# Making the low halves of every expert's weights on VectorE instead of sharing them with GpSimd

## The chip, the cores and the metric

The kernel runs on one core of a Trainium2 chip. The metric is the device time of one execution in microseconds (us). The core's engines run side by side and each works through its own instructions in order: TensorE (PE, with its weight loads shown as PEld), VectorE (DVE), ScalarE (ACT), GpSimd (POOL) and SyncE (SP), which issues most of the DMA transfers. GpSimd also issues the indirect transfers, that is the gathers and the scatter-additions by a list of rows.

## The reference, cut to what matters

The reference is one layer: two token mixers, then a mixture of experts, then a final norm. Only the experts bear on the change. 1024 tokens each go to 2 of 32 experts, and every expert is a SwiGLU of width 512 on rows of 1024:

```python
def expert_block(args):
    xb, e = args
    return (jax.nn.silu(xb @ w_gate[e]) * (xb @ w_up[e])) @ w_down[e]

y_buf = lax.map(expert_block, (x_buf, blk_e)).reshape(n_slots, d)
out = jax.ops.segment_sum(y_buf.astype(f32) * w_buf[:, None], tok_buf, num_segments=n_tok + 1)
```

All of it is in float32. Every expert's weights are read once, 6 MB each.

## The kernel before, in words

Up to about 690 us of the profile the kernel does the mixers, the output projection and the routing. What follows is the expert stage, and it ends at about 1330 us; the final norm comes last.

The stage walks 32 places, one expert each. Fifteen of them are **half experts**: they are given to experts that have at most 64 rows here, and their matmuls take the float32 weights as they came from memory (`half_gu` at L1263, `half_down` at L1287). One more half block rides along with place 13. The other seventeen places are **full experts** of 128 rows. From place 3 on, half and full ones mostly take turns. A full expert's product is made of three products of reduced-precision halves: a weight tile `wf` is split into a high part `wh` (ACT copies it, L181) and a low part `wl` (the source less the high part, L182), and PE multiplies high by high, high by low and low by high (`gu` at L1322, `down` at L1348). The rows `xT` and the hidden `hT` are split in the same way (L1312, L1341).

A full expert's weights come in twelve parts of 128 x 1024: parts 0 to 7 are gate and up, 8 to 11 are down. `chunk` (L1406 and on) hands one part out and has it split; `w_split` and `split` do it. In the kernel before, the low parts of 8 and 10 are made on POOL and all the others on DVE; `ON_POOL = (8, 10)` sets that, and the last place is left out of it. That is two instructions at each of 16 full experts, 32 in all. The tiles `wh` and `wl` have four buffers each, so a new part waits until PE has read the one four parts back.

Rows come in by a gather: POOL issues an indirect DMA that fills `xe` (L1239 for a full expert, L1234 for a half one), PE transposes it (`pxe`, L1309 and L1252) and ACT copies it out. `xe` has two buffers. The result `ye` or `yeh` (DVE, L1354 and L1292) is added into memory by another indirect DMA of POOL (L1358 and L1296). So POOL's queue in this stage holds, in an order that a scheduler fixes when the program is built: gathers, additions and the 32 low parts, and each waits for all before it. The order of `schedule` sets which step of which expert comes next; the scheduler then interleaves the engines' instructions by what it expects to be ready. DVE's queue holds the low parts, the products `hg` and `hgh` of the SwiGLU (L1330, L1270), the low halves of rows and hidden, a small helper for half experts' row numbers (`hrow`, L1202), and the results. SP loads the weights ahead into thirteen buffers of 1 MB, each as soon as one is free (L1218), and the row lists `lst` (L1200).

Of the kernel before, what the change touches and what calls it, by code (L numbers as in the profile page):

```python
# [25 lines left out]
NE = 32  # L26
# [34 lines left out]
H = 64  # L61

TS = NT + P

ON_POOL = (8, 10)


def ranks():
# [58 lines left out]
class Kern:  # L127
# [1282 lines left out]
    def chunk(self, p, part):  # L1410

        self.prefetch(len(self.order))
        c, h = self.part_of(part)
        f, s = self.F[p, c]
        if h:
            del self.F[p, c]
            self.live[s] -= 1
        f = f[:, h * D:(h + 1) * D]
        return f, None if self.half(p) else self.w_split(f, self.nc.gpsimd if part in ON_POOL and p < NE - 1 else None)

    def moe(self):
        blocks = list(range(MID + 1)) + [NE] + list(range(MID + 1, NE))
# [72 lines left out]
    def moe_rest(self):  # L1495
# [24 lines left out]
        with self.tc.For_i(0, n) as i:  # L1520
            ev, rv = self.ovf_regs(i)
            nc.sync.dma_start(out=lst, in_=self.tab[bass.ds(rv, P), :])
            self.gather(0, lst)
            x = self.x_t(0, (xh, xl), pt)
            for j in range(8):
                w = chunk(ev, j)
                self.gu(j // 2, x, w, w, pg, (j % 2,))
            h = self.act(pg, sg, hg)
            self.h_t(h, hT, pt)
            for f in range(4):  # L1530
                self.down(hT, chunk(ev, 8 + f), py, f)
            self.y_add(self.y_out(py, lst, y), lst)
# [193 lines left out]
```

## Time and profile before

| | |
|---|---|
| median of 3 runs | 1360.84 us (1359.11 to 1360.85) |
| the profiled execution | 1360.35 us |
| its span, first to last instruction | 1358.3 us |
| TensorE clock granted, mean | 0.94 |
| PE busy over the span | 1180.0 us (87%) |
| DVE busy | 842.5 us (62%) |
| ACT busy | 598.7 us (44%) |
| POOL busy | 430.7 us (32%) |

The profiled execution's own time is 2.05 us over its span; that is what lies before the first and behind the last instruction. It is 0.49 us below the median of the runs. Times in the views are us from the span's start. A row of a timeline gives the start, the length, the engine, the line, the operation and its tiles, and, in square brackets, how long the engine sat idle before it and what released it. Rows that follow each other with equal operations are merged (x2, x3). A row of the stretches gives each engine's busy time with its count of instructions, the granted TensorE clock as a share of full speed, the share of time the DMA engines were busy, and the rate of all transfers.

### The profile page before, as it was taken

What the parts mean: (1) busy time and instruction counts of PE and PEld (TensorE: products, weight loads), DVE (VectorE), ACT (ScalarE), POOL (GpSimd) and SP (SyncE); (2) the same over time, 40 slices, a digit from 0 to 9 for tenths busy, and PEclk for the clock granted to TensorE, in tenths of its full rate; (3) what the DMA queues carried; (4) which work ended last, traced back from release to release, by engine and by line L of the source; (5) the groups of instructions that cost most, each with busy time, mean ns of one, the idle gap of its engine ahead of it and who ended that gap; (6) DMA issues with size and microseconds to landing.
All of it is one profiled execution on the core that took longest, in us unless ns stands there. A gap on an engine that the chain in (4) does not pass through costs nothing. (4 is left out here: it accounts for less than half of the span.)

```text
span 1358.3 us, 18814 instructions
## 1 busy us (share of the span) xinstructions
PE 1180.0 (87%) x6628; PEld 859.1 (63%) x6628; DVE 842.5 (62%) x1364; ACT 598.7 (44%) x1064; POOL 430.7 (32%) x322
## 2 busy tenths in 40 slices
PE   5899999888888999899838999887999988898882
PEld 2678778788886666688726656454556655555552
DVE  1688884778858877556577754454555545454455
ACT  5633322455367766433425543332344333334344
POOL 0340001476523444013333431333332333332230
PEclk9699999979898999999968999899999989998996
DMA  9765645766223300873466999998689999988955
GB/s 333 252 207 167 209 136 160 248 195 213 93 79 121 109 9 16 298 260 130 167 224 228 347 387 406 367 347 323 240 328 402 398 357 327 376 339 319 342 176 231
DMA packets 104480, 335.02 MB, mean 247 GB/s; under 512 B 19532, under 2 KB 37964, under 8 KB 79808
## 3 DMA queue, kind: packets, MB, share of 16 engines
q1 hardware_dynamic: 94672, 314.78, 62.8%
q0 software_dynamic: 9136, 17.36, 5.2%
q10 hardware_dynamic: 576, 1.66, 0.3%
q8 instruction: 53, 0.87, 0.2%
q14 instruction: 43, 0.35, 0.1%
HBM read 299.74 MB, written 43.43 MB: 253 GB/s over the span
## 5 line engine op out<-in xcount | busy, mean ns | idle before, releaser
L182 DVE TENSOR_TENSOR wl<-wf,wh 128x1024 fp32r<-128x1024 f32 x172 | 255.8, 1518 | 121.4 <-ACT wh L181 121.2
L181 ACT CAST wh<-wf 128x1024 fp32r<-128x1024 f32 x204 | 204.7, 1050 | 146.5 <-PE pgu L1322 96.5
L1263 PE MATMUL pgu<-wf,xT 128*64 128x256 f32 x1024 | 136.0, 391 | 0.4 <-DVE yeh L1292 0.4
L182 POOL TENSOR_TENSOR wl<-wf,wh 128x1024 fp32r<-128x1024 f32 x32 | 87.3, 2738 | 84.7 <-ACT wh L181 74.1
L1322 PE MATMUL pgu<-wl,xh 128*128 128x512 f32 x272 | 98.1, 425 | 16.5 <-DVE wl L182 16.3
L1322 PE MATMUL pgu<-wh,xh 128*128 128x512 f32 x272 | 97.9, 434 | 9.9 <-ACT wh L181 9.8
L1263 PEld LDWEIGHTS pgu<-wf,xT 128*64 128x64 f32 x1024 | 72.0, 138 | 50.8 <-issue 16.4
L468 PE MATMUL pzq<-xw,hxh 128*128 128x256 f32 x512 | 100.1, 295 | 0.0
L770 POOL TENSOR_SCALAR p<-p,sst 128x640 f32<-128x640 f32 (+1 forms) x32 | 66.1, 2065 | 101.4 <-DVE sst L767 53.7
L1322 PE MATMUL pgu<-wh,xl 128*128 128x512 f32 x272 | 89.5, 410 | 0.0
L1348 PE MATMUL py<-wh,hT 128*128 128x512 f32 x272 | 83.5, 414 | 4.9 <-ACT hT L1340 3.1
L468 PEld LDWEIGHTS pzq<-xw,hxh 128*128 128x128 f32 x512 | 83.1, 196 | 1.0 <-issue 0.2
L1322 PEld LDWEIGHTS pgu<-wl,xh 128*128 128x128 f32 x272 | 54.1, 199 | 39.9 <-DVE wl L182 26.8
L1322 PEld LDWEIGHTS pgu<-wh,xh 128*128 128x128 f32 x272 | 51.2, 198 | 40.7 <-ACT wh L181 26.1
L349 PE MATMUL pxb<-hxh,xw 128*128 128x512 f32 x256 | 76.4, 397 | 0.0
L468 PE MATMUL pzq<-xw,hxl 128*128 128x256 f32 x256 | 74.2, 290 | 0.0
L1296 POOL DMA_INDIRECT acc<-yeh,hrow x16 | 34.6, 2160 | 121.2 <-DVE yeh L1292 102.8
L753 DVE TENSOR_REDUCE sst<-psc 128x1 f32<-128x640 f32 (+1 forms) x64 | 50.4, 789 | 27.7 <-PE psc L752 22.8
L1348 PEld LDWEIGHTS py<-wh,hT 128*128 128x128 f32 x272 | 49.7, 193 | 26.1 <-issue 6.7
L1287 PE MATMUL py<-wf,hTh 128*64 128x512 f32 x256 | 63.3, 614 | 0.9 <-ACT hTh L1280 0.9
L1322 PEld LDWEIGHTS pgu<-wh,xl 128*128 128x128 f32 x272 | 54.4, 200 | 13.4 <-issue 2.4
L1358 POOL DMA_INDIRECT acc<-ye,lst x16 | 35.0, 2185 | 87.5 <-DVE ye L1354 77.2
(348 smaller groups left out, 2559.1 us busy)
## 6 DMA issues: line engine op xcount, KB each, us to landing
wf<-in_w_gate SPq DMA_DIRECT2D x64, 1024.0 KB
wf<-in_w_up SPq DMA_DIRECT2D x64, 1024.0 KB
wf<-in_w_down SPq DMA_DIRECT2D x64, 1024.0 KB
wa<-in_w_ada SPq DMA_DIRECT2D x48, 512.0 KB
R<-csd SPq DMA_DIRECT2D x16, 512.0 KB
xl<-xd SPq DMA_DIRECT2D x17, 256.0 KB
xt<-in_x SPq DMA_DIRECT2D x8, 512.0 KB
xf<-in_w_xbc SPq DMA_DIRECT2D x8, 512.0 KB
```

Source lines behind the costliest of these rows:

```text
L181: self.nc.scalar.copy(hi, src)
L182: (eng or self.nc.vector).tensor_tensor(lo, src, hi.bitcast(F32), OP.subtract)
L349: nc.tensor.matmul(px[s], w(wp, kc), self.hx(hp, kc, s, 512), start=st, stop=sp)
L468: nc.tensor.matmul(ps, self.hx(hp, kc, b // 4, P, (b % 4) * P), w(wp, kc), start=kc == 0 and hp + wp == 0, stop=kc == KC - 1 and hp == 1)
L753: v.tensor_reduce(mx, ps[:, o:512 + nl], AX.X, OP.max)
L770: (v if j % 2 else nc.gpsimd).tensor_scalar(p_, p_, den[:, j - i:j - i + 1], None, op0=OP.mult)
L1263: self.nc.tensor.matmul(pg[n * H:n * H + H, o:o + 256], xT[:, i0 + kk, a * H:a * H + H], w[:, kk * 512 + n * 256:kk * 512 + n * 256 + 256] ...
L1287: self.nc.tensor.matmul(py[n * H:n * H + H, 0:512], hT[:, i, a * H:a * H + H], w[:, n * 512:n * 512 + 512], start=f == 0, stop=f == 3)
L1296: self.nc.gpsimd.indirect_dma_start(out=self.acc.rearrange("t (a c) -> (t a) c", a=2), out_offset=bass.IndirectOffsetOnAxis(ap=self.hrow[: ...
L1322: nc.tensor.matmul(pg[:, n * 512:(n + 1) * 512], x[xp][:, k, :], w[wp][:, kk * 512:(kk + 1) * 512], start=k == 0 and xp + wp == 0, stop=k ...
L1348: nc.tensor.matmul(py[:, n * 512:(n + 1) * 512], hT[:, hp, f, :], wd[wp][:, n * 512:(n + 1) * 512], start=f == 0 and hp + wp == 0, stop=f ...
L1358: self.nc.gpsimd.indirect_dma_start(out=self.acc[:, :], out_offset=bass.IndirectOffsetOnAxis(ap=lst[:, 0:1], axis=0), in_=y, in_offset=Non ...
```

## The change

`ON_POOL` goes, and every full expert's low parts are made on DVE:

```diff
-
-ON_POOL = (8, 10)
...
-        return f, None if self.half(p) else self.w_split(f, self.nc.gpsimd if part in ON_POOL and p < NE - 1 else None)
+        return f, None if self.half(p) else self.w_split(f)
```

`w_split` hands its `eng` on to `split`, which uses `self.nc.vector` when it is None. Two lines go at the top, so every line number of the changed kernel is lower by two. ACT's instructions keep their order, SP's differ by the place of one register load, and on PE a few of the rows' transposes move ahead by some matmuls. On POOL 32 instructions go; on DVE 32 come, and the scheduler places the others around them anew.

The first place is POOL, at one full expert between two half experts in the second half of the stage. Before, the queue holds a half expert's gather (`hrow`) and addition (`yeh`), the two low parts, the next full expert's gather (`lst`) and this one's addition (`ye`):

```order
L1234 DMA xe_6890<-h2d,hrow 128x512
L1296 DMA acc<-yeh,hrow 2304x512
L182 TENSOR_TENSOR wl<-wf,wh 128x1024 x2
L1239 DMA xe_6889<-h2d,lst 128x1024
L1358 DMA acc<-ye,lst 1152x1024
L1234 DMA xe_6890<-h2d,hrow 128x512
```

In the changed program the same place reads:

```order
L1232 DMA xe_6890<-h2d,hrow 128x512
L1294 DMA acc<-yeh,hrow 2304x512
L1237 DMA xe_6889<-h2d,lst 128x1024
L1356 DMA acc<-ye,lst 1152x1024
L1232 DMA xe_6890<-h2d,hrow 128x512
```

The full expert's gather has moved up: it now stands right behind the half expert's addition, with nothing between.

The second place is DVE, at the first full expert of the stage's second half, from a half expert's result (`yeh`) to the full expert's down parts. Before:

```order
L1292 SCALAR_TENSOR_TENSOR yeh<-py,lst,g2h 128x512
L182 TENSOR_TENSOR wl<-wf,wh 128x1024 x2
L1330 TENSOR_TENSOR hg<-sg,pgu 128x512
L182 TENSOR_TENSOR wl<-wf,wh 128x1024
L1341 TENSOR_TENSOR hT<-phT,hT 128x512
L182 TENSOR_TENSOR wl<-wf,wh 128x1024 x3
```

And in the changed program:

```order
L1290 SCALAR_TENSOR_TENSOR yeh<-py,lst,g2h 128x512
L180 TENSOR_TENSOR wl<-wf,wh 128x1024 x4
L1328 TENSOR_TENSOR hg<-sg,pgu 128x512
L180 TENSOR_TENSOR wl<-wf,wh 128x1024
L1339 TENSOR_TENSOR hT<-phT,hT 128x512
L180 TENSOR_TENSOR wl<-wf,wh 128x1024 x3
```

Parts 8 and 10 have come in ahead of `hg`, which now waits for four low parts where it waited for two.

## The prediction

> **What bounds the kernel now.** I read the page first, then the waits of PE in the expert stage, then the timelines of POOL, DVE and PE around the longest of them.
>
> ```profile
> PE 1180.0 (87%) x6628; PEld 859.1 (63%) x6628; DVE 842.5 (62%) x1364; ACT 598.7 (44%) x1064; POOL 430.7 (32%) x322
> ```
>
> PE is busiest by far, so a wait counts if PE sits in it. These are PE's own in the expert stage, 720 to 1350 us (total, times, longest):
>
> ```profile
> PE pxe L1309 <- DMA xe<-h2d,lst: 19.8, 8, 3.8
> PE pgu L1322 <- DVE wl L182: 13.1, 15, 1.3
> PE pgu L1322 <- ACT wh L181: 9.8, 7, 1.4
> PE phT L1338 <- DVE hg L1330: 6.7, 4, 2.9
> PE pxe L1252 <- DMA xe<-h2d,hrow: 4.4, 1, 4.4
> PE py L1348 <- POOL wl L182: 4.1, 7, 1.2
> ...
> PE py L1348 <- DVE hT L1341: 1.6, 4, 0.5
> ```
>
> The largest is not a weight part at all: eight times PE stands before a full expert's rows, which a gather of POOL brings. The next fences show why it is late, in the cycle from 1115 to 1160 us: POOL, then SP's load of the gather's row list, then the transposes on PE that read the rows.
>
> ```profile
> 1123.86 2.32 POOL L1296 DMA_INDIRECT acc<-yeh,hrow  x1 [7.76 <-DVE yeh L1292]
> 1132.05 5.76 POOL L182 TENSOR_TENSOR wl<-wf,wh 128x1024 fp32r<-128x1024 f32 x2 [5.87 <-ACT wh L181]
> 1137.95 1.86 POOL L1239 DMA_INDIRECT xe<-h2d,lst  x1
> ```
>
> ```profile
> 1097.72 0.33 SPq L1200 DMA_DIRECT2D lst<-tab  x1
> ...
> 1106.50 1.10 PE L1309 MATMUL pxe<-C,xe 128*128 128x128 f32 x4 [3.79 <-DMA xe<-h2d,lst]
> ...
> 1122.83 0.75 DVE L1292 SCALAR_TENSOR_TENSOR yeh<-py,lst,g2h 128x512 f32<-128x512 f32 x1 [4.74 <-PE py L1287]
> ...
> 1123.50 3.49 DVE L182 TENSOR_TENSOR wl<-wf,wh 128x1024 fp32r<-128x1024 f32 x3
> ```
>
> ```profile
> 1147.47 0.75 PE L1309 MATMUL pxe<-C,xe 128*128 128x128 f32 x4 [2.25 <-DMA xe<-h2d,lst]
> ```
>
> ```profile
> 1160.93 0.75 DVE L1292 SCALAR_TENSOR_TENSOR yeh<-py,lst,g2h 128x512 f32<-128x512 f32 x1 [4.65 <-PE py L1287]
> ```
>
> The gather is issued at 1137.95, the moment the two low parts are done; POOL had been idle for 5.87 us ahead of them, waiting for ACT's high parts. It takes 9.52 us until PE is released (1147.47 - 1137.95). Its buffer was read out by the transposes that start at 1106.50, and its list was asked for at 1097.72.
>
> **The change part by part.** *The gathers.* With the low parts gone, the gather stands right behind the addition, which ends at 1123.86 + 2.32 = 1126.18. Nothing else that it needs is later: the transposes that free the buffer begin 20 us before, and the list was asked for 28 us before. Landing 9.52 us on, it is there at 1135.70, and PE wants it at 1147.47 - 2.25 = 1145.22. The spare is 9.52 us, more than twice the longest wait of 3.8. Behind the gather in POOL's queue stand the addition and the next half expert's gather; each comes sooner, not later. I take all 19.8 us off; next late there is the high part from ACT, which PE waits for already (9.8 in all) and which stays.
>
> *The clock.* The granted clock falls after these waits. The stretches begin where PE resumes after a gather, except the second, which follows the wait for `hg`:
>
> ```profile
> core 0: us, PE busy (x) PEld busy (x) DVE busy (x) ACT busy (x) POOL busy (x), PEclk, DMA share, GB/s
> 865.00:877.00 12.00, 10.31 (x36) 6.50 (x37) 4.84 (x5) 5.20 (x6) 1.05 (x1) 0.72 0.91 331
> ...
> 1018.00:1025.00 7.00, 4.56 (x18) 2.87 (x19) 4.21 (x4) 0.59 (x1) 0.70 (x1) 0.76 1.02 418
> 1106.00:1118.00 12.00, 10.06 (x31) 6.16 (x31) 4.75 (x5) 5.20 (x6) 1.04 (x1) 0.59 0.78 297
> 1147.00:1159.00 12.00, 9.60 (x44) 6.11 (x44) 4.85 (x5) 5.37 (x7) 1.04 (x1) 1.00 0.98 345
> 1185.00:1197.00 12.00, 9.50 (x36) 5.77 (x37) 4.85 (x5) 5.20 (x6) 0.96 (x1) 0.86 0.91 325
> 1226.00:1238.00 12.00, 10.15 (x32) 6.40 (x33) 4.79 (x5) 5.20 (x6) 0.00 (x0) 0.61 0.93 335
> 1267.00:1279.00 12.00, 9.61 (x36) 5.84 (x37) 4.72 (x4) 5.20 (x6) 0.00 (x0) 0.86 1.02 377
> ```
>
> Clock lost behind gathers is 12 us times one less the clock: 3.4 + 4.9 + 1.7 + 4.7 + 1.7 = 16.4 us. Not all of it is time, since PE also waits there for parts. The same work, from the transposes to `yeh`, took 1122.83 - 1106.50 = 16.33 us at a clock of 0.59 and 1160.93 - 1147.47 = 13.46 at 1.00: 2.87 us for 4.9 us of lost clock, a ratio of 0.59. So 16.4 x 0.59 = 9.6 us. The bounds are nothing (the halving comes back behind other waits) and 16.4.
>
> The Trainium skill (TensorE: Matmul & The Clock Gate, Part 1: The HAM clock gate) says the clock halves after an idle window of about 3.4 us. By that only the waits of 3.79 and the one at 1226 would cost clock, and this term would be (4.9 + 4.7) x 0.59 = 5.6 us, the sum 4 us less; the row at 1185 speaks against it, for the clock fell there too.
>
> *The low parts.* On DVE a low part costs 1.22 us where POOL is quiet, and beside POOL it stands still:
>
> ```profile
> 1009.89 1.22 DVE L182 TENSOR_TENSOR wl<-wf,wh 128x1024 fp32r<-128x1024 f32 x1
> 1014.38 5.40 DVE L182 TENSOR_TENSOR wl<-wf,wh 128x1024 fp32r<-128x1024 f32 x1 [3.27 <-ACT wh L181]
> 1019.71 0.68 DVE L1330 TENSOR_TENSOR hg<-sg,pgu 128x512 f32<-128x512 f32 x1
> ```
>
> ```profile
> 1013.97 4.73 POOL L182 TENSOR_TENSOR wl<-wf,wh 128x1024 fp32r<-128x1024 f32 x2
> ```
>
> ```profile
> 1015.10 1.05 ACT L181 CAST wh<-wf 128x1024 fp32r<-128x1024 f32 x1 [0.74 <-PE pgu L1322]
> ```
>
> ```profile
> L182 DVE TENSOR_TENSOR wl<-wf,wh 128x1024 fp32r<-128x1024 f32 x164 | 246.1, 1532 | 121.4 <-ACT wh L181 121.2
> ...
> L182 POOL TENSOR_TENSOR wl<-wf,wh 128x1024 fp32r<-128x1024 f32 x32 | 87.3, 2738 | 84.7 <-ACT wh L181 74.1 <-issue 10.5
> ```
>
> One DVE part took 5.40 us while POOL made two in 4.73. Over the stage DVE's mean is 1532 ns, 0.31 us over 1.22, so 164 x 0.31 = 51 us of DVE time is standing beside POOL. The change adds 32 x 1.22 = 39 us to DVE and takes up to 51 off. For PE what counts is when the down parts are ready: POOL's pair takes 5.76 us, all four on DVE 4 x 1.22 = 4.88. So the 4.1 us that PE waits for POOL's parts goes, and what would be late next, the hidden's low half (1.6), is no later; I count its gain as nothing, 1.6 at most.
>
> *`hg`.* It now stands behind four low parts at two full experts. At the first of these, the last of the four needs ACT's part, done at 1015.10 + 1.05 = 1016.15; then 1.22 and 0.68 give 1018.05, against 1019.71 + 0.68 = 1020.39 before. That is 2.3 us of the 2.9 us wait, and the 7 us stretch behind it lost 1.7 us of clock, x 0.59 = 1.0. Nothing to 6.7 bounds it with its like.
>
> *The rest.* The half expert's gather (4.4) waits for `hrow` on DVE; I leave it, with 0 to 4.4 as bounds. The three full experts in a row at the start are where DVE is fullest:
>
> ```profile
> 720.00:770.00 50.00, 46.45 (x207) 34.63 (x205) 38.05 (x31) 31.89 (x37) 21.98 (x11) 0.97 0.82 299
> ...
> 838.00:960.00 122.00, 103.59 (x522) 64.73 (x523) 58.53 (x53) 44.16 (x58) 41.13 (x20) 0.96 0.94 352
> ```
>
> ```profile
> 1014.00:1090.00 76.00, 72.16 (x387) 46.48 (x386) 43.66 (x40) 32.25 (x43) 24.31 (x12) 0.98 1.02 398
> 1100.00:1262.00 162.00, 139.17 (x682) 88.23 (x680) 78.70 (x73) 59.74 (x76) 53.12 (x24) 0.93 0.91 340
> ```
>
> In 720 to 770 DVE would go from 38.05 to at most 38.05 + 6 x 1.22 = 45.4, just under PE's 46.45: nothing, 7.3 us of loss at worst. From 1100 on DVE has 83 of 162 us free.
>
> Sum: 19.8 + 9.6 + 4.1 + 2.3 + 1.0 = 36.8 us off the profiled execution's 1360.35 us, which is 0.5 below the median: 1323.5, said as 1323.
>
> **The rivals.** *The gather stays late* (0.12). DVE now runs low parts closer together while POOL prepares its transfers, or the gather meets the addition's own transfer ahead of it. Beside DVE's three parts the addition at 1123.86 took 2.32 us. The delay decides only beyond the 9.52 us of spare, and the run of DVE parts that could hold it is four, 4.88 us. If it does, 19.8 + 9.6 are lost: 1360.35 - 7.4 = 1353.
>
> *The weight stream becomes the bound* (0.10). From 1100 to 1262 transfers move 340 GB/s x 162 us = 55.1 MB. My terms there, the waits before 1106.50, 1147.47 and two more of that size, some 12 us, and 11.3 x 0.59 = 6.7 of clock, leave 143 us, so 385 GB/s are wanted. The row from 1014 to 1090 held 398 at a share of 1.02, for 76 us. If only the midpoint of 340 and 398 is kept, 369, the stretch takes 149, 6 us more; 838 to 960, with 352 already, loses about as much: 1323.5 + 12 = 1335, up to 1340. The Trainium skill (SBUF — State Buffer, A bandwidth-pool intuition that's wrong (but worth ruling out)) gives about 358 GB/s from memory to a core; by it the stretch would take 154 us and the sum come to some 1340. The measured 398 decides against it.
>
> *DVE sets the pace* (0.04), the slower side. If two more low parts per full expert make the down parts late, each costs 1.22 on PE's path: 32 x 1.22 = 39 us and, with the gather gain failing, 1399. It decides where four DVE parts take longer than POOL's pair, that is above 5.76 / 4 = 1.44 us each. Rows without POOL show 1.22, and DVE's 83 free us speak against it.
>
> *Nothing comes of it* (0.04). The low parts are gone from POOL, so the change does what it says; but the gained time could be given back at the next wait for high parts: 1360.
>
> **How the numbers follow.** The forecast has 0.70. Its own range, with the clock term from 0 to 16.4, the other waits' bounds and a small part of the 7.3, is 1311 to 1333. The stream rival carries the upper end to 1340; outside are the late gather, DVE's pace and nothing, together 0.20. A measurement of this kernel can tell about 0.2%, 2.7 us, from no change. Faster: 0.70 + 0.12 + 0.10 = 0.92; same 0.04; slower 0.04.
>
> **What would show it.** In the changed profile: DVE's low parts x196 in the stage at a mean near 1.22 us, none on POOL; the wait of the transposes for the gathered rows near zero; the clock at 1.00 behind them; the second half of the stage at a DMA share near 1.0. Wrong would be a wait for rows that stays, a new wait of PE for low parts above 13.1 us, or high parts waiting for weights.

## The result, and the profile after

The changed kernel takes 1315.54 us in the median of 4 runs (1313.18 to 1322.09). The kernel before, run beside it, takes 1359.97 us (1352.35 to 1360.85). The ratio is 0.9694, with a 95% interval of 0.9655 to 0.9734. The profiled execution takes 1317.32 us at a span of 1315.2 us, against 1360.35 and 1358.3: 43.0 us less, where the prediction's sum said 36.8. In the changed file the lines behind the removed two are two lower: the low part is L180, the high part L179, the gather of a full expert L1237, its transposes L1307.

The page of the changed kernel, busy times:

```profile
PE 1164.3 (89%) x6628; PEld 853.0 (65%) x6628; DVE 828.8 (63%) x1396; ACT 598.2 (45%) x1064; POOL 341.2 (26%) x290
```

DVE has 32 instructions more and is busy 13.7 us less (842.5 before). How, the groups of instructions show; DVE's low parts from 720 to 1310 us of the changed kernel (count, busy, mean in ns):

```profile
L180 DVE TENSOR_TENSOR wl<-wf,wh 128x1024 fp32r<-128x1024 f32 x195 | 230.8, 1220 | 85.6 <-ACT wh L179 82.3 <-DMA wf<-in_w_down 2.4
```

195 low parts at a mean of 1220 ns; before, 164 took 1532 ns each. Now PE's waits in the same stretch (total, times, longest):

```profile
PE pgu L1320 <- DVE wl L180: 13.7, 17, 1.3
PE pgu L1320 <- ACT wh L179: 10.0, 8, 1.4
PE pxe L1250 <- DMA xe<-h2d,hrow: 3.6, 1, 3.6
...
PE phT L1336 <- DVE hg L1328: 2.8, 1, 2.8
...
PE pxe L1307 <- DMA xe<-h2d,lst: 0.4, 1, 0.4
```

The wait for a full expert's rows, 19.8 us in eight pieces before, is 0.4 us in one. No wait for POOL's low parts is left, and none of the hidden's low half. The waits for `hg` within the stage are gone, all 3.9 us of them; the 2.8 us that stays belongs to the last expert, and before had it too. What stays much as it was are the waits for high parts (10.0 us for 9.8) and for DVE's low parts (13.7 for 13.1).

POOL of the changed kernel, in one of the pairs of a half and a full expert:

```profile
1131.74 2.32 POOL L1294 DMA_INDIRECT acc<-yeh,hrow  x1 [4.41 <-DVE yeh L1290]
1134.37 1.41 POOL L1237 DMA_INDIRECT xe<-h2d,lst  x1 [0.30 <-issue]
```

PE of the changed kernel in the same pair, at the transposes of those rows:

```profile
1152.60 0.75 PE L1307 MATMUL pxe<-C,xe 128*128 128x128 f32 x4
...
1156.02 0.50 PE L1320 MATMUL pgu<-wh,xh 128*128 128x512 f32 x1 [1.41 <-ACT wh L179]
...
1157.28 0.50 PE L1320 MATMUL pgu<-wl,xh 128*128 128x512 f32 x1 [0.52 <-DVE wl L180]
```

The gather now stands 2.63 us behind the addition, where it stood 14.09 us behind it (1137.95 - 1123.86). The transposes come 18.23 us later, far more than the 9.52 us that a gather took, and PE does not wait.

To see where the 43 us lie, the stage is cut at instructions that both kernels have: the second half expert's gather, the last addition before the first one of a half expert, the addition of a `yeh` ahead of the last five pairs, and the same one behind them. The stretches of the kernel before (length, busy times with counts, granted clock, DMA share, GB/s):

```profile
721.04:779.84 58.80, 54.73 (x252) 39.88 (x253) 41.75 (x34) 34.30 (x39) 23.64 (x12) 0.97 0.85 313
779.84:1081.87 302.03, 274.41 (x1442) 170.51 (x1439) 152.98 (x143) 115.39 (x149) 95.29 (x49) 0.98 0.93 355
1081.87:1283.50 201.63, 173.36 (x847) 108.91 (x845) 97.73 (x89) 75.06 (x96) 65.14 (x29) 0.93 0.93 350
1283.50:1358.30 74.80, 45.21 (x207) 30.37 (x207) 43.57 (x46) 32.07 (x52) 14.27 (x7) 0.84 0.58 202
```

And of the changed kernel:

```profile
719.56:773.72 54.16, 52.86 (x256) 39.48 (x257) 41.61 (x41) 34.30 (x39) 9.09 (x6) 1.00 0.92 339
773.72:1060.15 286.43, 270.29 (x1435) 169.94 (x1432) 145.22 (x156) 115.39 (x149) 56.48 (x36) 0.98 0.95 368
1060.15:1241.75 181.60, 167.24 (x850) 106.30 (x848) 93.35 (x99) 75.04 (x96) 33.83 (x20) 0.97 1.02 393
1241.75:1315.20 73.45, 45.24 (x207) 30.60 (x207) 42.27 (x48) 32.06 (x52) 8.75 (x5) 0.84 0.62 220
```

| stretch | before | after | change | the prediction's terms that lie there |
|---|---|---|---|---|
| ahead of it | 721.04 | 719.56 | -1.5 | 0 |
| three full experts in a row | 58.80 | 54.16 | -4.6 | -1.2 |
| middle | 302.03 | 286.43 | -15.6 | -11.6 |
| last five pairs | 201.63 | 181.60 | -20.0 | -22.8 |
| rest | 74.80 | 73.45 | -1.3 | -1.3 |

The waits for POOL's parts (4.1) are put where they stood, 1.2, 0.8, 0.8 and 1.3 from the three full experts on. The 1.5 us ahead come before any low part of POOL, so they are scatter between executions. Behind that the scatter is small: of the kernels below, the one with POOL's parts at the first three experts and the one with POOL at work beside DVE keep the changed order in the last five pairs, and took 181.50 and 181.78 us for them, against 181.60.

PE's matmuls are 2748 over the four stretches in both kernels. They kept it busy for 547.7 us before (54.73 + 274.41 + 173.36 + 45.21) and for 535.6 after, 12.1 less; the other 29.5 of the 41.6 us are time in which PE no longer stands. In the last five pairs all transfers together ran at 393 GB/s, with the DMA engines busy throughout.

### The profile page after: what moved, and what is told of

The parts are those of the page before. It is cut to its first block, busy times and chain, and to the rows that moved or that the text cites. A ratio compares the mean times of both kernels' runs of the same rounds, so it can differ in the third digit from the quotient of the medians.

```text
span 1315.2 us, 18760 instructions
## 1 busy us (share of the span) xinstructions
PE 1164.3 (89%) x6628; PEld 853.0 (65%) x6628; DVE 828.8 (63%) x1396; ACT 598.2 (45%) x1064; POOL 341.2 (26%) x290
## 5 line engine op out<-in xcount | busy, mean ns | idle before, releaser
L180 DVE TENSOR_TENSOR wl<-wf,wh 128x1024 fp32r<-128x1024 f32 x204 | 241.7, 1220 | 86.0 <-ACT wh L179 82.6
L179 ACT CAST wh<-wf 128x1024 fp32r<-128x1024 f32 x204 | 204.8, 1050 | 136.3 <-PE pgu L1320 95.9
L1320 PEld LDWEIGHTS pgu<-wh,xl 128*128 128x128 f32 x272 | 53.6, 197 | 13.3 <-issue 2.4
L1309 ACT CAST xh<-pxe 128x512 fp32r<-128x512 f32 x34 | 19.5, 589 | 93.7 <-PE pgu L1320 57.5
```

The costliest lines, as they stand in the source:

```text
L179: self.nc.scalar.copy(hi, src)
L180: (eng or self.nc.vector).tensor_tensor(lo, src, hi.bitcast(F32), OP.subtract)
L1320: nc.tensor.matmul(pg[:, n * 512:(n + 1) * 512], x[xp][:, k, :], w[wp][:, kk * 512:(kk + 1) * 512], start=k == 0 and xp + wp == 0, stop=k ...
```

## The experiments

Theory: the gather's place in POOL's queue is worth most of the gain, because PE waits for the rows and the clock falls behind that wait. Rival: POOL's low parts cost the time by themselves, by making DVE stand still and PE wait for their results. A second rival is the weight stream, which the prediction held ready as a new bound. Times of different calls are compared by their ratio to the kernel before, run beside them; 0.001 is 1.36 us. Line numbers are those of each run's own file. The stretches come from one profiled execution of each kernel.

**The gather ahead, in the kernel before.**

```diff
                 st += [("gu", p, j)]
+                if p > REST and not apart and j == 0:
+                    st += [("x", p)]
...
-                if j == 2:
+                if j == 2 and (p <= REST or apart):
                     st += [("x", p)]
```

> The kernel before, with POOL's low parts kept, but the transposes of the next full expert's rows, and with them the gather behind them, written ahead of the down parts; in the last five cycles POOL then issues the gather before its two low parts. Theory (the gather's place in POOL's queue is what counts): the last five waits for gathered rows (3.79, 2.25, 2.26 and two of that size, 14.3 us together) and the clock lost behind them go, 20 to 25 us faster than before, about 1337. Rival (what counts is DVE standing beside POOL and PE waiting for POOL's parts, which this keeps): within 5 us of 1360.

Measured: 1348.82 us, ratio 0.9923 (0.9883 to 0.9962), some 10 us faster: between the theory's 20 to 25 and the rival's 5. The profiled execution (1355.55 us) is one of its longer ones; its last five pairs fell by 3.2 us only:

```profile
1081.76:1280.19 198.43, 175.59 (x857) 111.62 (x855) 101.90 (x90) 75.16 (x95) 63.45 (x30) 0.93 0.96 362
```

POOL and then PE of this kernel show why:

```profile
1161.24 1.40 POOL L1239 DMA_INDIRECT xe<-h2d,lst  x1 [0.31 <-PE pgu L1322]
1168.83 5.72 POOL L182 TENSOR_TENSOR wl<-wf,wh 128x1024 fp32r<-128x1024 f32 x2 [6.19 <-ACT wh L181]
```

```profile
1172.93 0.60 PE L1309 MATMUL pxe<-C,xe 128*128 128x128 f32 x3 [2.79 <-DMA xe<-h2d,lst]
```

The gather is early, but the transposes moved with it. They want the rows at 1172.93 - 2.79 = 1170.14, 11.5 us behind the addition at 1158.61; in the kernel before it was 1145.22 - 1123.86 = 21.4. The edit takes ahead the step that makes the transposes, with the gather behind them, so the lead was gone. The experiment does not separate the theories.

**The gather held back, in the changed kernel.** One wait is added and no instruction moves (`self.late` is the last down part's low part):

```diff
+        if b is not None and b > REST:
+            self.tc.add_manual_dep(g.ins, self.late.ins.name, ...)
```

> The changed kernel, all low parts on DVE, but from block 15 on each gather of a full expert's rows is made to wait for the low part of the last down part of the full expert before. No instruction changes its place. In the changed kernel that low part ends about 11 us behind the addition (1107.8 against 1096.9), so the gather, 9.5 us long, would land at 1117.4 where PE wants the rows at 1115.4. Theory (the gather's place): five waits for rows of about 2 us come back, 10 us, and with the clock behind them 10 to 24 us slower than the changed kernel, 1326 to 1340. Rival (low parts of POOL are the cost, whatever the gather does): no slower than 1318.

Measured: 1333.25 us, ratio 0.9825 (0.9763 to 0.9886), 17.7 us slower than the changed kernel, within the theory's 10 to 24. POOL, PE and the last five pairs of this kernel:

```profile
1139.88 2.32 POOL L1296 DMA_INDIRECT acc<-yeh,hrow  x1 [3.76 <-DVE yeh L1292]
1153.95 1.04 POOL L1237 DMA_INDIRECT xe<-h2d,lst  x1 [11.74 <-PE py L1348]
```

```profile
1162.76 0.75 PE L1309 MATMUL pxe<-C,xe 128*128 128x128 f32 x4 [1.93 <-DMA xe<-h2d,lst]
```

```profile
1063.37:1256.51 193.14, 165.63 (x851) 106.11 (x849) 93.34 (x99) 75.05 (x96) 32.35 (x20) 0.97 0.99 374
```

The gather is again 14.07 us behind the addition, as in the kernel before, though POOL does nothing meanwhile. PE waits for rows again, and the five pairs take 11.5 us more than in the changed kernel. Its waits there, and below them those of the kernel before:

```profile
PE pxe L1309 <- DMA xe<-h2d,lst: 13.3, 5, 4.0
```

```profile
PE pxe L1309 <- DMA xe<-h2d,lst: 14.3, 5, 3.8
```

So the late gather costs time without any low part on POOL; the rival's "no slower than 1318" falls. Its clock, though, is 0.97, as in the changed kernel: these waits brought no clock loss that shows in the five pairs.

**A third buffer for gathered rows.** It lets the gather be written ahead of the down parts while the transposes stay where the program has them:

```diff
-        self.xe = [self.mp([D], "xe%d" % k) for k in range(2)]
+        self.xe = [self.mp([D], "xe%d" % k) for k in range(3)]
...
                 st += [("gu", p, j)]
+                if p > REST and p in HALVES and not apart and j == 0:
+                    st += [("rows", p)]
```

("rows" issues the gather that "x" issued; the index is taken modulo three.) It was made twice, from the kernel before:

> The kernel before, POOL's low parts kept. A third buffer for gathered rows lets the gather of a full expert be written ahead of the down parts without moving the transposes; in the last five cycles POOL issues it ahead of its two low parts, in the earlier cycles its place hardly changes. Theory (the gather's place): the last five waits for rows, 14.3 us, go. In the kernel with the late gather the same waits cost 11.5 us in these cycles, so 11 to 20 us faster than before. Rival (POOL's low parts cost the time whatever the gather does, as the first experiment's 3 us in these cycles would have it): within 5 us of before.

and from the changed kernel:

> The changed kernel with the same third buffer and the same early gather, as the control of the third buffer. Theory (in the changed kernel the gather comes early enough already): within 3 us of the changed kernel, 1315.5. Its distance to the kernel before with a third buffer is then what POOL's low parts cost beside the gather's place: 43 less the 11 to 20 of that run, if the terms add up.

Measured: from the kernel before 1343.47 us, ratio 0.9884 (0.9849 to 0.9919), 15.8 us faster, as the theory had it. From the changed kernel 1328.22 us, ratio 0.9756 (0.9722 to 0.979), 8 to 13 us slower than the changed kernel (by ratio and by median; the intervals overlap a little) instead of equal, so as a control it did not hold. The last five pairs, first with POOL's low parts, then without:

```profile
1068.45:1262.08 193.63, 176.94 (x859) 110.28 (x857) 96.18 (x90) 77.44 (x98) 61.54 (x30) 0.94 0.98 372
```

```profile
1061.33:1252.93 191.60, 174.97 (x859) 110.22 (x857) 95.20 (x100) 77.47 (x98) 35.25 (x19) 0.95 1.00 382
```

PE's waits in these pairs, with the third buffer and POOL's low parts:

```profile
PE pgu L1322 <- ACT wh L181: 7.0, 5, 1.4
PE pgu L1322 <- DVE wl L182: 6.4, 8, 1.1
PE pxe L1309 <- ACT xT L1253: 2.6, 5, 0.5
PE py L1348 <- POOL wl L182: 0.4, 1, 0.4
```

The wait for rows is gone, as meant. But the scheduler placed the transposes otherwise, and five waits for ACT's copy `xT` came in; with less clock as well (0.95 against 0.97) that order costs 191.60 - 181.60 = 10.0 us where nothing else differs in kind. Against one another the two differ by POOL's low parts, with the gather early in both: 2.0 us in the five pairs. From before to the early gather it is 8.0 us in spite of the order's 10.0, so 18.0 for the gather's place, if the order costs the same in both, which is not shown.

**POOL's low parts at the first three full experts alone**, in the kernel before:

```diff
-        ... self.nc.gpsimd if part in ON_POOL and p < NE - 1 else None)
+        ... self.nc.gpsimd if part in ON_POOL and p < FIXED else None)
```

> Two low parts of each of the first three full experts alone stay on POOL, six of the 32; all other low parts are on DVE. The additions of POOL in that stretch came 4.6 us earlier with the change, where the prediction counted nothing. Theory (DVE standing beside POOL and PE waiting behind it is that gain): 4 to 6 us slower than the changed kernel, about 1320. Rival (the early gain belongs to something else, or is given back at the next wait): within 2 us of the changed kernel, 1315.5.

Measured: 1322.69 us, ratio 0.9734 (0.9689 to 0.9779), some 5 to 7 us slower than the changed kernel; the intervals overlap, but the profile puts it in one place:

```profile
720.57:780.27 59.70, 55.05 (x252) 40.25 (x253) 41.84 (x35) 34.30 (x40) 23.17 (x12) 0.97 0.84 307
780.27:1067.01 286.74, 270.28 (x1439) 170.14 (x1436) 146.27 (x157) 115.42 (x149) 56.33 (x35) 0.98 0.96 368
```

The first stretch is 5.5 us longer than in the changed kernel (54.16), and the next one 0.3. So that gain belongs to POOL's low parts there, where no wait for gathered rows stands. The groups of DVE's low parts there, before from 720 to 780 us and in the changed kernel from 720 to 774:

```profile
L182 DVE TENSOR_TENSOR wl<-wf,wh 128x1024 fp32r<-128x1024 f32 x23 | 35.7, 1585 | 8.4 <-ACT wh L181 8.4
```

```profile
L180 DVE TENSOR_TENSOR wl<-wf,wh 128x1024 fp32r<-128x1024 f32 x29 | 34.1, 1219 | 6.4 <-ACT wh L179 6.1
```

Six parts more on DVE take 1.6 us less in sum, since each of the 23 that were there loses 0.37 us.

**POOL at work beside DVE, without the gather being late**, in the changed kernel:

```diff
+        for v in range(2 if b is not None and b > REST else 0):
+            t = self.mp([D], "idle", 1)
+            v = self.nc.gpsimd.tensor_tensor(t, self.g2, self.g2, OP.subtract)
...
```

> The changed kernel; from block 15 on, right behind each gather of a full expert's rows, POOL makes two subtractions of the size of a low part, of constants, into a tile that nobody reads. The gather is as early as in the changed kernel, no engine waits for these results, and all low parts stay on DVE. Theory (DVE standing beside POOL costs time by itself, beside the gather's place; in the last five cycles the kernel before took 8.5 us more than the kernel with the late gather, whose waits for rows were as long): 5 to 15 us slower than the changed kernel, 1320 to 1331. Rival (only the gather's place counts): within 3 us of 1315.5.

Measured: 1318.39 us, ratio 0.9706 (0.9677 to 0.9735), within 3 us of the changed kernel, and the five pairs are equal to 0.2 us:

```profile
1067.06:1248.84 181.78, 167.41 (x851) 106.50 (x849) 93.31 (x99) 75.06 (x96) 52.87 (x30) 0.97 1.02 393
```

The expected 5 to 15 us did not come. It is a weak test all the same: behind the gather these subtractions rarely met DVE's low parts, whose mean from 945 us on was 1263 ns, against 1221 in the changed kernel and 1512 in the kernel before. What it shows is that POOL's work at this place costs nothing, not that standing beside it never does.

**The splits ahead.** What PE still waits for are high parts (10.0 us) and DVE's low parts (13.7). This edit takes the splits of the next full expert ahead of the half expert's activation and output on ACT and DVE:

```diff
-            st += [("act", p)]
+            pre = lambda q, *k: [("pre", q, i) for i in k] if q < NE and q not in HALVES and p in HALVES else []
+            st += pre(p + 1, 0, 1) + [("act", p)] + pre(p + 1, 2)
...
-                    st += down[2:4] + [("y", p - 1)]
+                    st += down[2:4] + ([("pre", p, 4), ("pre", p, 5)] if p - 1 in HALVES and p not in HALVES else []) + [("y", p - 1)]
```

("pre" calls `chunk` for that part; the half expert's activation, product and output are also ordered behind the splits that were written ahead of them.)

> The changed kernel; behind a half expert, the first two weight parts of the full expert that follows are split by ACT and DVE ahead of the half expert's activation, and two more ahead of its scaling of the output (yeh). Same instructions, same bytes, another order on ACT and DVE. It aims at the waits of PE that are left: 1.41 us for a high part, 0.53 and 1.08 for low parts in each pair of half and full expert, of 10.0 and 13.7 us in all. Theory (after the change the order of the splits limits the stage, and the stream of weights has room): 10 to 25 us faster than the changed kernel, 1291 to 1306. Rival (the stream, at 393 GB/s there, is the bound): within 5 us of 1315.5.

Measured: 1307.39 us, ratio 0.9628 (0.9598 to 0.9659), 8 to 9 us faster than the changed kernel, between the two. The five pairs take 10.3 us less, at full clock:

```profile
1049.75:1221.04 171.29, 162.47 (x861) 105.11 (x860) 95.05 (x100) 75.58 (x96) 32.38 (x20) 1.00 1.01 393
```

But late in the stage PE stands for 9.5 us. ACT, then PE:

```profile
1242.64 1.04 ACT L179 CAST wh<-wf 128x1024 fp32r<-128x1024 f32 x1 [10.59 <-DMA wf<-in_w_gate]
```

```profile
1249.59 0.70 PE L1277 MATMUL phT<-C,hgh 128*128 128x128 f32 x2 [9.51 <-DVE hgh L1269]
```

ACT waits 10.59 us for a weight load with the half expert's activation queued behind it. So the stream does become late, in a kernel whose pairs are shorter, and the splits put ahead hand that wait on to work that needed no weights.

**The same, without the last full expert:**

```diff
-            pre = lambda q, *k: [("pre", q, i) for i in k] if q < NE and q not in HALVES and p in HALVES else []
+            pre = lambda q, *k: [("pre", q, i) for i in k] if q < NE - 1 and q not in HALVES and p in HALVES else []
```

> The kernel with the splits ahead, but the last full expert's splits stay where the changed kernel has them, behind the last half expert's activation, since there ACT stood 10.6 us for a weight load with the half expert's work queued behind it (PE waited 9.5 us for hgh). Theory (the stream is late only there, and PE can do the half expert's work in that time): 4 to 9 us faster than the kernel with all splits ahead, 1298 to 1303. Rival (the stream sets the pace of the whole second half, and the wait only moves): within 3 us of 1307.

Measured: 1301.01 us, ratio 0.9563 (0.9531 to 0.9596), 6 to 9 us less (by median and by ratio), as the theory had it.

**And without expert 13** (of whose splits parts 4 and 5 stay ahead):

```diff
-            ... if q < NE - 1 and q not in HALVES and p in HALVES else []
+            ... if q < NE - 1 and q != MID and q not in HALVES and p in HALVES else []
```

> The kernel with the splits ahead except at the last full expert, and now also except at expert 13, where it lost 5 us against the changed kernel between two additions of POOL (39.2 us against 34.1) and PE waited 4.0 us for hgh. Theory (there, as at the end, the splits stood in front of the half expert's work and waited for weights): 3 to 6 us faster than that kernel, 1295 to 1298. Rival (the stream gives it back at the next waits): within 2 us of 1301.

Measured: 1296.11 us, ratio 0.9542 (0.9509 to 0.9575). By the medians it is 5 us less, as the theory had it; by the ratios 3, and the intervals overlap. This is the fastest kernel of the study that does all the work, about 20 us below the changed one, with the same instructions and bytes. Its last five pairs:

```profile
1050.51:1219.17 168.66, 162.46 (x858) 104.81 (x858) 94.78 (x100) 75.58 (x96) 33.03 (x19) 1.00 1.02 395
```

The queue that brings the weights (and the small row lists) in the five pairs of the changed kernel, then of this one (packets, MB, share of the DMA engines):

```profile
q1 hardware_dynamic: 10142, 65.02, 88.4%
```

```profile
q1 hardware_dynamic: 9509, 60.42, 87.5%
```

Over 181.60 and 168.66 us that is 358 GB/s in both. So shorter pairs did not draw the weights faster: 4.6 MB less came in them, and as much more behind them. The ten experts of these pairs need 60 loads of 1 MB, 62.9 million bytes, so some 2.5 MB of them must have been loaded ahead.

**Half the bytes of each weight load** behind the first thirteen, in the changed kernel:

```diff
-        self.nc.sync.dma_start(out=f, in_=self.w_src(e, c))
+        n = 2 * D if self.fn < NL + NR else D
+        self.nc.sync.dma_start(out=f[:, 0:n], in_=self.w_src(e, c)[:, 0:n])
...
+        h = h if self.order.index((p, c)) < NL + NR else 0
```

The second half of such a load is left out, and the parts that would come from it are made from the first half. An earlier form, in which these parts still read the second half, gave no time; of that form a time within 3 us of the changed kernel was expected if the stream is not the bound, and a gain of 6 or more if it is.

> The changed kernel, but each weight load behind the first thirteen of the expert stage moves only the first half of its bytes, and the parts of the second half are made from the first half, so the expert outputs are not the reference's. The scheduler, which counts a load by its bytes, then also picks another order of the splits, so this bounds both together. Theory (the stream is not the bound; the order of the splits is): faster than 1315.5, and not by more than 25 us. Rival (the stream sets the pace of the stage's second half): faster by 40 us or more, since the stage would fall to PE's own 90 per cent.

Measured: 1271.59 us, ratio 0.9374 (0.9339 to 0.9408), 44 us less than the changed kernel. Its last five pairs:

```profile
1033.30:1191.17 157.87, 157.87 (x851) 104.99 (x850) 96.41 (x100) 77.28 (x95) 33.77 (x20) 1.00 0.78 240
```

PE is busy all the time there. By the numbers expected, the rival is right: with the order that it brings about, the byte count is worth more than 40 us. But it holds two things, fewer bytes and another order, and the kernel with the splits ahead had 20 us with all bytes. So neither alone is shown to be the bound of the changed kernel. In the five pairs the order gives 12.9 us (181.60 to 168.66) at 395 GB/s, and at most another 10.8 would come from half the bytes. How much of that is the bytes and how much the order was not separated.

## Why the prediction was right, point by point

**The gathers (19.8 us): right.** The waits for rows fell by 19.4 us, the gather went out 2.63 us behind the addition, and the spare was enough. Holding it back alone brought 14.0 us of waits over the stage and 13 us of stage (11.5 in the last five pairs, 1.5 in the middle, from 286.43 to 287.94); there a late gather cost about its waits.

**The clock behind them (9.6 us, with `hg` 10.6): the step was wrong in its mechanism, and its size fits by luck.** The prediction priced each wait for rows with a clock loss that would go with it. Lost clock, length times one less the clock, in the first three stretches is 1.8 + 6.0 + 14.1 = 21.9 us before and 0 + 5.7 + 5.4 = 11.1 after. 10.8 us went, where 16.4 + 1.7 = 18.1 were counted; times 0.59 that would be 6.4. But PE's busy time for as many matmuls fell by 12.1 us, where 10.6 were forecast, and its idle time by 29.5, where the waits in the sum are 26.2. If the clock is all of the 12.1, which is not shown, less of it came back than counted and each us was worth more than 0.59, so that two errors about cancel. And the kernel with the late gather has the waits back with a clock of 0.97 in the last five pairs. Two stretches of the changed kernel, each of 12 us from transposes that did not wait:

```profile
1152.00:1164.00 12.00, 10.03 (x49) 6.14 (x44) 5.27 (x6) 6.06 (x8) 2.04 (x2) 1.00 1.02 377
1188.00:1200.00 12.00, 10.02 (x40) 6.16 (x37) 5.27 (x6) 6.06 (x8) 0.95 (x2) 0.86 1.01 371
```

PE's waits in the second of them (those in the first are shown above):

```profile
1191.69 0.50 PE L1320 MATMUL pgu<-wh,xh 128*128 128x512 f32 x1 [1.41 <-ACT wh L179]
...
1192.95 0.79 PE L1320 MATMUL pgu<-wl,xh 128*128 128x512 f32 x1 [0.53 <-DVE wl L180]
```

The waits are the same; one stretch lost clock and the other did not, so a wait has no fixed price in clock. It is not chance of one execution: behind the same two sets of transposes the kernel with POOL's parts at the first three experts and the one with POOL at work beside DVE were granted 1.00 and 0.86 too. What decides it is not shown. The Trainium skill (TensorE: Matmul & The Clock Gate, Part 1: The HAM clock gate) says the window over which the clock's gate watches PE, some 3.4 us, runs freely, and that the number of slow matmuls depends on its phase; by that these two rows can differ as they do. An idle window of 3.4 us without any instruction is not what the second row shows, since its longest wait is 1.41; ten small transposes and one matmul stand ahead of that wait, and whether they count as work for the clock no run here tells. Of the prediction's signs, the clock at 1.00 behind the transposes came only in part.

**PE's waits for POOL's low parts (4.1): right.** None is left.

**`hg` (2.3): too small, within its bounds.** All 3.9 us of the waits in the middle went.

**The three full experts in a row (0 beside 1.2 of waits for POOL, and a loss up to 7.3 as its worst): too small, and the bound on the wrong side.** The working added six parts of 1.22 us to DVE's 38.05 and took nothing off for the 23 parts that stood beside POOL, though its own paragraph on the low parts had the number for the whole stage (0.31 us each). They got 0.37 us shorter, 8.4 us in all; DVE's busy time stayed (41.75 to 41.61) and the stretch fell by 4.6 us. PE's waits in it went from 3.7 us (1.2 for POOL's part, 0.9 for DVE's, 0.7 for the hidden's low half, 0.9 for its high half) to that last 0.9, and its busy time fell by 1.9. The run with POOL's parts only there put back 5.5.

**The middle: 15.6 for 11.6.** Beside `hg` these terms were taken as nothing and brought something: the hidden's low half 0.9 us and the half expert's gather 0.8, within the bounds given, and `hgh` 1.0, for which none was given.

**The last five pairs: 20.0 for 22.8.** What the place of the gather is worth there lies between 11.5 us (taken back in the changed kernel) and 18.0 (brought forward in the kernel before); the remaining 2.0 to 8.5 belong to POOL's low parts. Why the ends don't meet stays open. One part may be the clock, 0.93 to 0.97 in these kernels: the kernel before and the one with the late gather have nearly the same waits for rows (14.3 and 13.3) but lost 14.1 and 5.8 us of clock. Why the clock falls further beside POOL's low parts is not shown.

**The rivals.** The gather did not stay late, and DVE did not set the pace: 1220 ns per part, as forecast. The stream did not set the pace: PE waited for no load, and ACT waited for none in the last five pairs. But it came closer than the forecast's 0.10 makes it seem. All transfers ran at 393 GB/s there, more than the 385 asked for and near the 398 of the row from 1014 to 1090, and the kernels with the splits ahead, whose pairs are 10 to 13 us shorter, got 393 and 395. At 395, the most that a run held over these pairs, the 71.3 MB that the changed kernel moved in these pairs (393 x 181.60) take 180.5 us, an estimate that leaves it 1 us. The order of the splits was still worth 20 us, part of it from loads made ahead, and with it mended a load is late.

**The signs of being wrong.** Two showed faintly: PE's waits for low parts are 13.7 us, above the 13.1 named, and ACT waited 7.7 us for weight loads over the stage where it had waited 3.6. Neither cost what it stood for, since PE's waits for high parts stayed at 10.0.

## What to carry to other kernels

Before a queue's work is priced by its busy time, look at what stands behind it: two subtractions, 5.76 us together, held back a transfer of 9.52 us on which PE waited. When work moves off an engine that shares something with another, take off the other's slow-down everywhere where you add the moved instructions, not only in the sum over the stage. And an experiment that moves a transfer forward must hold its consumer in place; a wait added in the faster kernel, with no instruction moved, gave the cleaner answer.

## What the runs showed of the hardware

The clock's price was not expected: two stretches alike in work and waits were granted 0.86 and 1.00, and waits for rows of 13.3 and 14.3 us went with 0.97 and 0.93 in the last five pairs. All transfers together kept 393 to 395 GB/s for 169 to 182 us on end, of which the weight loads' queue had 358, and single slices of the changed kernel's page, 33 us long, stand at 412:

```profile
GB/s 338 251 201 184 211 137 133 255 194 215 154 69 100 139 31 9 118 355 178 120 248 169 311 374 412 406 394 380 307 229 412 395 405 405 389 389 386 360 203 224
```

The Trainium skill (SBUF — State Buffer, A bandwidth-pool intuition that's wrong (but worth ruling out)) gives some 358 GB/s between memory and a core; these rows, of all transfers, do not agree with it.
